# Seven of the eight token-to-channel turns of the input projection taken off TensorE: VectorE 32x32 blocks and a trip through DRAM

## The chip, the core and the metric

The kernel runs on one core of a Trainium2 chip. The metric is the device time of one execution in microseconds (us); before the change the median of three runs is 1167.25 us (1164.77 to 1167.39). Engines are named as in the profile: PE (TensorE matmul), PEld (its weight loads), DVE (VectorE), ACT (ScalarE), POOL (GpSimd), SP (the engine whose queue issues the loads and stores here).

## The reference

One encoder layer on 256 tokens of width 2048, fp32. The part that the change touches is the mixing sub-layer:

```python
hn = rms_norm(h, g_mix_pre)
u = hn @ w_in                                   # 2048 -> 5120
q, k, v, xr, yg = split(u, [1024, 2048, 3072, 4096])
attn = neighborhood_attention(q, k, v, rpb)     # 8 heads of 128, 4 rows x 64 columns of tokens
rec = rglru_bidirectional(xr, ...) * gelu(yg)   # conv of 4 taps, two gates, two scans
mixed = concat(rms_norm(attn), rms_norm(rec)) @ w_out
h = h + rms_norm(mixed)
```

Behind it come a SwiGLU FFN (2048 to 5632 and back) and a gated embedding, each with its norms.

## The kernel before, in words

Every product runs on PE in three passes (`hi*hi`, `hi*lo`, `lo*hi`), since each fp32 operand is split in two parts: ACT rounds the weight tile `wr` to `wh` (L472), DVE subtracts to get `wl` (L501). A weight tile holds 2 x 128 rows and 512 columns and feeds twelve matmuls of 512 columns (L539 to L541 in `products`). There are four raw weight buffers and six pairs `wh`, `wl`, so ACT and DVE can be several tiles ahead of PE.

The input projection is ten chunks of 512 columns, eight weight tiles each, with tokens on the partitions of the result `acc`. Their order was X0, V0, Q0, K0, X1, V1, Q1, K1, G0, G1 (x for the recurrence, v, q, k, and the gate; two halves of each). When a chunk is done, its `post` function runs beside the next chunks: `evac` scales `acc` by the norm into the one buffer `ev` (ACT, L791). x, q, k and the gate are needed with channels on the partitions, and `transposed` does that with four PE transposes into one PSUM bank (L321), two such sets for a chunk. Then:

- x: ACT copies the turned data into `xp` with the tokens in row order (L808); `rec_unit` works on two blocks of 128 channels at a time, four units in all, called units 0 to 3 here (0 and 1 from X0, 2 and 3 from X1). A unit loads its gate weights into `av` (`load_gates`, L821) and splits them (`gh` on ACT L301, `gl` on DVE L303), does eight convolution instructions on DVE (L844, L849: four taps, two blocks), splits the result `xc` (`xch` ACT, `xcl` DVE), and then PE multiplies it by the gate weights (`pg`, two groups of twelve matmuls, L325 to L327). Sigmoids, exponentials, scans and the sum `hs` (L888) follow, and the next unit begins.
- q, k: split into `qh`, `ql`, `kh`, `kl` (L301, L303); then the heads' scores `sc` on PE.
- gate: multiplied into `hs` (L956).

The program is one list for each engine, executed in order. Its order is made by the planner `Plan` while the kernel is built: each piece of work is a generator that yields an engine and an estimated cost, and the piece that could start first is placed next. PE pieces are placed between half weight tiles of the main products, when the planner holds their inputs to be ready. A piece that is late on the chip holds its engine, and so whatever stands behind it.

In the FFN another way of turning is already in use (`Gated.turn`, L1608 to L1645): DVE transposes 32x32 blocks in place, one DMA writes the result to a DRAM buffer `via`, four DMAs read it back with the blocks exchanged, all from SP's queue.

Of the kernel before, what the change touches and what calls it, by code (L numbers as in the profile page):

```python
# [16 lines left out]
P = 128  # L17
# [22 lines left out]
C_RG = 8.0  # L40

# [19 lines left out]
ADDED = 3.0  # L61
LANDED = 6.0
SHARED = 2.6
# [30 lines left out]
class Plan:  # L94
# [13 lines left out]
    def __init__(self, **slots):  # L108
        self.clk = {"act": 0.0, "dve": 0.0, "pe": 0.0, "dma": 0.0, "sum": 0.0}
# [123 lines left out]
def added(kb):  # L233
    return ("sum", kb / 512 * ADDED, None, None, None)


# [5 lines left out]
def layer(ctx: ExitStack, tc: tile.TileContext, a: dict, out: bass.AP):  # L242
# [4 lines left out]
    ps = ctx.enter_context(tc.tile_pool(name="ps", bufs=4, space=bass.MemoryType.PSUM))  # L247
    plan = Plan(
# [74 lines left out]

    def mm3(o, lh, ll, rh, rl, start, stop, shared=False):
# [56 lines left out]
    singles, sums, by_dma = {}, {}, set()  # L381

    class Group:


        def __init__(self, w, n0, lhs, ks, kinds, post, after=None):
# [5 lines left out]
            for (k, _), kind in self.units:  # L392
                i = len(tiles)
                tiles.extend((w[c], k, n0[c]) for c in range(2))
                by_dma.update(i + n for n in {"d": (0, 1), "e": (1,), "c": (0,), "t": (0,)}.get(kind, ()))
                if kind in "st":
# [59 lines left out]
    def hi_stream():  # L456
        for i in range(len(tiles)):
# [16 lines left out]
            if i in by_dma:  # L474
                yield act(2 * N)
                nc.scalar.activation(los[i], f32(his[i]), AF.Copy, scale=-1.0)
                plan.add(add_raw(i), plan.now)

    def add_to(out, src, kb):
        yield added(kb)  # L480
        plan.clk["dma"] = max(plan.clk["dma"], plan.now - ADDED) + SHARED * kb / 512
        nc.gpsimd.dma_start(out, src, accum_op=ALU.add)
        landed = Event()
        landed.t = plan.now + LANDED
        yield landed

    def add_raw(i):
        yield from add_to(los[i], raws[i], 512)
        done(ev_lo[i, 2])
        used(i)  # L490

    def lo_stream():
        for i in range(len(tiles)):
            if i in by_dma:
                continue
# [83 lines left out]
    def run_group(g, flip):  # L579
# [5 lines left out]
        strassens = [n for n, (_, kind) in enumerate(g.units) if kind in "st"]  # L585
        for n, ((_, kx), kind) in enumerate(g.units):
            if kind in "st":
# [153 lines left out]
    def open_p1():  # L741
# [5 lines left out]
        xp = p1.tile([P, HB, S + 4], F32, name="xp")  # L747
        nc.gpsimd.memset(xp[:, :, 0:2], 0.0)
        nc.gpsimd.memset(xp[:, :, S + 2 : S + 4], 0.0)
# [25 lines left out]
    HB = 4  # L775
# [7 lines left out]
    def evac(ch, func, tables):  # L783
# [3 lines left out]
        for t in range(NT):  # L787
            yield act(N, tables, take="ev" if t == 0 else None)
            if e is None:
                e = t1["pool"].tile([P, NT, N], F32, tag="ev", name="ev")  # L790
            nc.scalar.activation(e[:, t, :], ch.accs[t], func, scale=rstd_x[:, t : t + 1])  # L791
        release(ch)
        return e
# [3 lines left out]
    def xr_post(hf):  # L797
        def post(ch):
# [32 lines left out]
    def rec_unit(b0, xp):  # L831
# [7 lines left out]
        for b in range(2):  # L839
            for j in range(4):  # L840
                w = col("conv_w", j * 8 + b0 + b)
                yield dve(S)
                if j == 0:
                    nc.vector.tensor_scalar(  # L844
                        out=xc[:, b, :], in0=xp[:, b, 0:S], scalar1=w,
                        scalar2=col("conv_b", b0 + b), op0=ALU.mult, op1=ALU.add,
                    )
# [101 lines left out]
    def gate_pair(b0, b, e, ev):  # L949
        hs, sq = t1["hs"], t1["sqr", b // 2]  # L950
        tr = yield from transposed(e, b)
        if b == 2:
            plan.free["ev"].append(plan.now)
        h2 = hs[:, b0 + b : b0 + b + 2, :]
        yield dve(2 * S, give="sm")
        nc.vector.tensor_tensor(out=h2, in0=tr, in1=h2, op=ALU.mult)  # L956
# [5 lines left out]
    def yg_post(hf):  # L962
        def post(ch):
            b0 = hf * HB
            e = yield from evac(ch, AF.Gelu_apprx_tanh, GELU)
# [3 lines left out]
            both = [Event() for _ in range(2)]  # L969
            for i in range(2):  # L970
                plan.add(gate_pair(b0, 2 * i, e, both[i]), plan.now)
# [27 lines left out]
    def qk_post(g, which):  # L999
        def post(ch):  # L1000
# [5 lines left out]
            for b in range(0, HB, 2):  # L1006
                tr = yield from transposed(e, b)
                if b == 2:
                    plan.free["ev"].append(plan.now)
                yield from split(hi[:, b : b + 2, :], lo[:, b : b + 2, :], tr, 2 * S, give="sm")  # L1010
# [153 lines left out]
    O_Q, O_K, O_V, O_X, O_G = 0, DA, 2 * DA, 3 * DA, 3 * DA + DR  # L1164
# [205 lines left out]
    kept = ctx.enter_context(tc.tile_pool(name="kept", bufs=1, space=bass.MemoryType.DRAM))  # L1370

# [182 lines left out]
    def quarters(x):  # L1554
        return x.rearrange("p (c n) -> p c n", n=P)

# [29 lines left out]
    class Gated(Seven):  # L1586
# [5 lines left out]
        def late(self, g):  # L1592
# [13 lines left out]
            yield dve(2 * N)  # L1606
            turned = self.both.rearrange("p c t n -> p (c t n)")
            nc.vector.transpose(turned, turned)  # L1608
            plan.free["uv"].append(plan.now)
            if not self.kk0:  # L1610
                self.mid.open()
            raw = self.mid.raw
            there = Event()
            plan.add(self.turn(raw, there), plan.now, TURN_LATE)
            yield there
            i, j = divmod(self.kk0, 8)
            hi, lo = (x[:, j : j + 4, :].rearrange("p b (t a i) -> p t a b i", t=NT, i=32)
                      for x in self.mid.tiles(i))
            raw = raw.rearrange("p a t (b i) -> p t a b i", i=32)
# [10 lines left out]

        def turn(self, raw, there):
            yield dma(512)
            via = kept.tile([P, 4, NT * P], F32, tag="via", name="via", bufs=2)
            nc.sync.dma_start(via, self.both.rearrange("p c t n -> p c (t n)"))
            out = Event()
            out.t = plan.now + VIA
            yield out
            plan.free["mid"].append(plan.now)
            yield dma(512)
            for c in range(4):  # L1640
                nc.sync.dma_start(
                    raw[c * 32 : (c + 1) * 32].rearrange("j a t n -> j a (t n)"),
                    via[:, c, :].rearrange("(a j) n -> j a n", a=4),
                )
            there.t = plan.now + VIA  # L1645
# [45 lines left out]
    for part, (f0, f1) in enumerate(parts):  # L1691
# [4 lines left out]
        for us in units[:1] if last else units:  # L1696
            summed += [k for kind, k in us if kind in "st" and k not in summed]
# [201 lines left out]
```

## Time and profile before

| | |
|---|---|
| median of three runs | 1167.25 us (1164.77, 1167.25, 1167.39) |
| profiled execution: its time | 1164.49 us |
| profiled execution: its span, first to last instruction | 1162.7 us |
| granted TensorE clock, mean | 0.997 |
| PE busy in the span | 98% |
| DVE, ACT busy in the span | 81%, 60% |

The span is the profiled execution of one program; the time holds some 1.8 us more around it. A busy PE is a PE with matmuls in flight: one 512-column matmul is listed with some 390 ns, but the next one starts some 227 ns after it, and this distance is the cost of one. What PE waits for is read from the list of waits, where a wait is put down to the engine that ended it.

### The profile page before, as it was taken

The page shows a single profiled execution, that of the slowest core. Times are in us where ns is not written, and L with a number is a line of the kernel's source. Part 1 is how long each engine was busy: PE and PEld are TensorE (multiplying, and loading weights), DVE is VectorE, ACT ScalarE, POOL GpSimd, SP SyncE. Part 2 cuts the span into 40 slices and gives each one's busy share as a digit, 9 for nine tenths or more (in the row PEclk, how much of TensorE's full clock was granted, in tenths as well). Part 3 has the DMA queues.
Part 4 walks back from the last instruction along what each step waited for, and adds up shares of the span by engine and source line. Part 5 has one row for each costly group of instructions (what it writes and reads, how often), then busy time and mean ns, then how long its engine had stood idle before and what let it go on. Part 6 is the DMA issues. An engine that isn't in the chain of part 4 may idle for free.

```text
span 1162.7 us, 14552 instructions
## 1 busy us (share of the span) xinstructions
PE 1144.1 (98%) x5189; PEld 948.0 (82%) x5189; DVE 942.7 (81%) x1214; ACT 692.2 (60%) x927; POOL 1.6 (0%) x13
## 2 busy tenths in 40 slices
PE   7999999999999999999999999999999999999996
PEld 5888888888888888888888888888888888888885
DVE  6677868778548889899877889989977999987663
ACT  6787877766547645565454555556444546466752
POOL 0000000000000000000000000000000000000000
PEclk9999999999999999999999999999999999999998
DMA  9855565545874967677765676677675667975741
GB/s 311 288 172 184 170 195 183 163 156 171 314 252 142 319 206 239 231 234 240 232 216 171 224 222 199 203 232 255 211 240 177 209 201 216 331 268 168 247 145 73
DMA packets 78265, 250.34 MB, mean 215 GB/s; under 512 B 8433, under 2 KB 20337, under 8 KB 76785
## 3 DMA queue, kind: packets, MB, share of 16 engines
q1 hardware_dynamic: 78048, 249.33, 65.4%
q8 instruction: 41, 0.67, 0.2%
q14 instruction: 32, 0.25, 0.1%
q10 hardware_dynamic: 144, 0.08, 0.0%
HBM read 238.37 MB, written 11.01 MB: 214 GB/s over the span
## 4 chain that ended last, share of the span: by engine, by line
PE 92%; DVE 3%; ACT 2%; DMA 2%; SPq 1%; issue 1%; DVEq 0%; ACTq 0%
PE c L539 14%; PE c L541 14%; PE c L540 14%; PE acc L541 11%; PE acc L540 11%; PE acc L539 11%; PE p L548 3%; PE p L550 3%; PE p L549 3%; PE c L548 2%; PE c L549 2%; PE c L550 2%; DMA av<-in_w_rg_i 1%; DVE wl L501 1%; PE tr L321 1%; ACT wh L472 1%
## 5 line engine op out<-in xcount | busy, mean ns | idle before, releaser
L501 DVE TENSOR_TENSOR wl<-wr,wh 128x1024 fp32r<-128x1024 f32 (+1 forms) x319 | 368.1, 1170 | 87.7 <-ACT wh L472 87.1
L472 ACT CAST wh<-wr 128x1024 fp32r<-128x1024 f32 (+1 forms) x319 | 317.3, 1012 | 164.8 <-PE acc L541 70.5
L539 PE MATMUL c<-wh,hT_mix_hi 128*128 128x512 f32 x436 | 170.1, 390 | 0.0
L541 PE MATMUL c<-wh,hT_mix_lo 128*128 128x512 f32 x436 | 169.7, 389 | 0.0
L540 PE MATMUL c<-wl,hT_mix_hi 128*128 128x512 f32 x436 | 169.6, 389 | 0.0
L472 ACT CAST wh<-lent_t 128x1024 fp32r<-128x1024 f32 x65 | 68.0, 1053 | 117.8 <-DVE lent_t L525 84.4
L539 PE MATMUL acc<-wh,hT_hi 128*128 128x512 f32 x320 | 128.5, 402 | 6.7 <-ACT wh L472 6.7
L540 PE MATMUL acc<-wl,hT_hi 128*128 128x512 f32 x320 | 126.2, 394 | 0.8 <-DVE wl L501 0.8
L541 PE MATMUL acc<-wh,hT_lo 128*128 128x512 f32 x320 | 126.1, 394 | 0.0
L541 PEld LDWEIGHTS c<-wh,hT_mix_lo 128*128 128x128 f32 x436 | 81.8, 188 | 17.2 <-DVE hT_mix_lo L309 0.2
L539 PEld LDWEIGHTS c<-wh,hT_mix_hi 128*128 128x128 f32 x436 | 81.9, 188 | 16.8
L540 PEld LDWEIGHTS c<-wl,hT_mix_hi 128*128 128x128 f32 x436 | 81.9, 188 | 16.7
L501 DVE TENSOR_TENSOR wl<-lent_t,wh 128x1024 fp32r<-128x1024 f32 x65 | 78.1, 1219 | 13.5 <-ACT wh L472 13.2
L472 ACT CAST wh<-lent_r 128x1024 fp32r<-128x1024 f32 (+1 forms) x61 | 58.8, 981 | 32.5 <-PE c L541 25.6
L539 PEld LDWEIGHTS acc<-wh,hT_hi 128*128 128x128 f32 x320 | 61.0, 191 | 18.4 <-ACT wh L472 6.7
L501 DVE TENSOR_TENSOR wl<-lent_r,wh 128x1024 fp32r<-128x1024 f32 (+1 forms) x61 | 68.3, 1129 | 8.3 <-ACT wh L472 8.2
L540 PEld LDWEIGHTS acc<-wl,hT_hi 128*128 128x128 f32 x320 | 60.9, 190 | 13.8 <-DVE wl L501 2.2
L541 PEld LDWEIGHTS acc<-wh,hT_lo 128*128 128x128 f32 x320 | 60.8, 190 | 12.9
L541 PE MATMUL acc<-wh,hT_ffn_lo 128*128 128x512 f32 x112 | 43.7, 390 | 0.4 <-DVE hT_ffn_lo L309 0.4
L539 PE MATMUL acc<-wh,hT_ffn_hi 128*128 128x512 f32 x112 | 44.1, 393 | 0.0
L540 PE MATMUL acc<-wl,hT_ffn_hi 128*128 128x512 f32 x112 | 43.6, 389 | 0.0
L539 PE MATMUL c<-wh,mid1h 128*128 128x512 f32 x88 | 34.2, 389 | 0.0
(440 smaller groups left out, 2219.1 us busy)
## 6 DMA issues: line engine op xcount, KB each, us to landing
wr<-in_w_in SPq DMA_DIRECT2D x79, 512.0 KB, 4.3
wr<-in_w_ffn_down SPq DMA_DIRECT2D x70, 512.0 KB, 4.6
wr<-in_w_ffn_gate SPq DMA_DIRECT2D x64, 512.0 KB, 4.6
wr<-in_w_ffn_up SPq DMA_DIRECT2D x64, 512.0 KB, 4.2
wr<-in_w_out SPq DMA_DIRECT2D x32, 512.0 KB, 4.7
wr<-in_w_ple_gate SPq DMA_DIRECT2D x32, 512.0 KB, 4.5
lent_r<-in_w_ffn_up SPq DMA_DIRECT2D x24, 512.0 KB, 4.7
lent_r<-in_w_ffn_gate SPq DMA_DIRECT2D x24, 512.0 KB, 4.5
```

The costliest lines, as they stand in the source:

```text
L321: nc.tensor.transpose(tr[:, b, t * P : (t + 1) * P], src, ident)
L472: nc.scalar.copy(his[i][:, j, :], raws[i][:, j, :])
L501: nc.vector.tensor_tensor(out=los[i][:, j, :], in0=raws[i][:, j, :], in1=f32(his[i][:, j, :]), op=ALU.subtract,)
L539: nc.tensor.matmul(accs[t], hi[t], wh[:, j, :], start=st, stop=False)
L540: nc.tensor.matmul(accs[t], hi[t], wl[:, j, :], start=False, stop=False)
L541: nc.tensor.matmul(accs[t], lo[t], wh[:, j, :], start=False, stop=sp)
L548: nc.tensor.matmul(o, lh, wh, start=start, stop=False)
L549: nc.tensor.matmul(o, lh, wl, start=False, stop=False)
L550: nc.tensor.matmul(o, ll, wh, start=False, stop=stop)
```

## The change

x, q, k and the first gate half (G0) are turned as in the FFN. `evac` now writes `ev` in quarters of 128 columns; `turned` adds one DVE block transpose of 128x1024; `turn` adds the write to `via` and four reads back into `ev`, on SP's queue. The columns of `w_in` are permuted on the host in 32s, so that the exchange comes out right. One ACT copy or split of 1024 elements then reads `ev` in place of two of 512 that read PSUM. In `xp` the tokens stay in column order; the convolution taps are shifted by `j * NR`, two small DVE copies fill the edges between rows, and the convolution writes `xc` in row order itself, which makes `xc` a strided operand (neighbours 64 elements apart, runs of four). G1 and the heads' own transposes stay on PE. V1 now stands behind Q1 and K1. Code for a kind of tile that no table uses (`by_dma`, `added`) is removed, and the planner's `LANDED` goes from 6.0 to 2.5.

```diff
+    def turned(e, raw, read, free=None):
+
+        yield dve(2 * N)
+        flat = e.rearrange("p c t n -> p (c t n)")
+        nc.vector.transpose(flat, flat)
+        plan.add(turn(e, raw, read, free), plan.now, TURN_LATE)
+
+    def turn(e, raw, read, free):
+        yield dma(512)
+        via = kept.tile([P, 4, NT * P], F32, tag="via", name="via", bufs=2)
+        nc.sync.dma_start(via, e.rearrange("p c t n -> p c (t n)"))
+        out = Event()
+        out.t = plan.now + VIA
+        yield out
...
+        yield dma(512)
+        for c in range(4):
+            nc.sync.dma_start(
+                raw[c * 32 : (c + 1) * 32].rearrange("j a t n -> j a (t n)"),
+                via[:, c, :].rearrange("(a j) n -> j a n", a=4),
+            )
+        read.t = plan.now + VIA
...
-            for b in range(0, HB, 2):
-                tr = yield from transposed(e, b)
-                if b == 2:
-                    plan.free["ev"].append(plan.now)
-                yield act(2 * S, give="sm")
-                nc.scalar.copy(
-                    xp[:, b : b + 2, 2 : S + 2].rearrange("p b (r c) -> p b r c", r=NR),
-                    tr.rearrange("p b (c r) -> p b r c", r=NR),
+            yield act(4 * S)
+            nc.scalar.copy(by_block(xp[:, :, LEFT : LEFT + S]), e)
...
+                to = xc[:, b, :].rearrange("p (r c) -> p c r", r=NR)
+                src = xp[:, b, j * NR : j * NR + S].rearrange("p (c r) -> p c r", r=NR)
...
                     nc.vector.scalar_tensor_tensor(
-                        out=xc[:, b, :], in0=xp[:, b, j : j + S], scalar=w, in1=xc[:, b, :],
-                        op0=ALU.mult, op1=ALU.add,
+                        out=to, in0=src, scalar=w, in1=to, op0=ALU.mult, op1=ALU.add,
                     )
...
-            for b in range(0, HB, 2):
-                tr = yield from transposed(e, b)
-                if b == 2:
-                    plan.free["ev"].append(plan.now)
-                yield from split(hi[:, b : b + 2, :], lo[:, b : b + 2, :], tr, 2 * S, give="sm")
+            yield from split(by_block(hi), by_block(lo), e, 4 * S, give="ev")
...
         (O_X, xr_post(0)), (O_V, v_post(0)), (O_Q, qk_post(0, "q")), (O_K, qk_post(0, "k")),
-        (O_X + N, xr_post(1)), (O_V + N, v_post(1)), (O_Q + N, qk_post(1, "q")),
-        (O_K + N, qk_post(1, "k")), (O_G, yg_post(0)), (O_G + N, yg_post(1)),
+        (O_X + N, xr_post(1)), (O_Q + N, qk_post(1, "q")),
+        (O_K + N, qk_post(1, "k")), (O_V + N, v_post(1)), (O_G, yg_post(0)), (O_G + N, yg_post(1)),
```

What the planner makes of it is seen in the order of the instructions. On PE, before, in the second chunk (V0, its result is `acc_363` and `acc_364`), the two sets that turn X0 stand between matmuls of the main product:

```order
L541 MATMUL acc_364<-wh,hT_lo 128x512
L321 MATMUL tr<-ident,ev 128x128 x4
L539 MATMUL acc_363<-wh,hT_hi 128x512
L540 MATMUL acc_363<-wl,hT_hi 128x512
L541 MATMUL acc_363<-wh,hT_lo 128x512
L539 MATMUL acc_364<-wh,hT_hi 128x512
L540 MATMUL acc_364<-wl,hT_hi 128x512
L541 MATMUL acc_364<-wh,hT_lo 128x512
L321 MATMUL tr<-ident,ev 128x128 x4
```

After the change these sets are gone, and so are those of X1, Q0, Q1, K0, K1 and G0: fourteen sets. The first gate group `pg` of unit 0 stands behind 21.5 weight tiles, where it stood behind 17.5 (counted in PE's order); here it is in the new order, in the third chunk (Q0):

```order
L550 MATMUL acc_554<-wh,hT_lo 128x512
L354 MATMUL pg<-xch,gh 128x256
L355 MATMUL pg<-xcl,gh 128x256
L356 MATMUL pg<-xch,gl 128x256
```

On DVE, in the new order, between the first convolution of unit 1 and its gate weights stand a block transpose (that of K0) and a weight split:

```order
L867 TENSOR_SCALAR xc<-xp,vec 128x64x4
L872 SCALAR_TENSOR_TENSOR xc<-xp,vec,xc 128x64x4
L327 STREAM_TRANSPOSE ev<-ev 128x1024
L872 SCALAR_TENSOR_TENSOR xc<-xp,vec,xc 128x64x4 x2
L867 TENSOR_SCALAR xc<-xp,vec 128x64x4
L872 SCALAR_TENSOR_TENSOR xc<-xp,vec,xc 128x64x4 x2
L510 TENSOR_TENSOR wl<-wr,wh 128x1024
L872 SCALAR_TENSOR_TENSOR xc<-xp,vec,xc 128x64x4
L299 TENSOR_TENSOR gl<-av,gh 128x1024
L299 TENSOR_TENSOR xcl<-xc,xch 128x512
```

Before, the same place held the eight convolutions, one weight split, `gl` and `xcl`; what moved in is the transpose, and the convolutions have the strided form.

On SP's queue, in the new order, the trip of Q0 stands between weight loads, and behind it come the gate weights of unit 1:

```order
L333 DMA via<-ev 128x1024
L475 DMA wr<-in_w_in 128x1024 x2
L341 DMA ev<-via 32x4x256 x4
L475 DMA wr<-in_w_in 128x1024 x5
L842 DMA av<-in_w_rg_a 128x2x128
```

Before, there was no `via` on this stretch of the queue. Behind the first half of the output projection PE's, ACT's and DVE's instructions stand in the same order as before.

## Rows read from the trace of the kernel before

**Rows 1.** The page's first part: busy time, share of the span, instructions.

```profile
PE 1144.1 (98%) x5189; PEld 948.0 (82%) x5189; DVE 942.7 (81%) x1214; ACT 692.2 (60%) x927; POOL 1.6 (0%) x13
```

**Rows 2.** Windows, the stretch of the input projection and the first tiles behind it.

```profile
core 0: us, PE busy (x) PEld busy (x) DVE busy (x) ACT busy (x) POOL busy (x), PEclk, DMA share, GB/s
9.60:290.00 280.40, 278.71 (x1354) 232.74 (x1354) 214.59 (x323) 206.80 (x315) 0.00 (x0) 1.00 0.61 197
```

**Rows 3.** Waits of PE: line and who ended them, us in total, times, longest.

```profile
PE acc L539 <- ACT wh L472: 6.7, 1, 6.7
PE pg L326 <- DVE xcl L303: 0.9, 3, 0.5
PE acc L540 <- DVE wl L501: 0.8, 1, 0.8
```

**Rows 4.** Timeline of PE: start, duration, instruction; one transposing set of X0.

```profile
47.70 0.39 PE L540 MATMUL acc<-wl,hT_hi 128*128 128x512 f32 x1
47.93 0.39 PE L541 MATMUL acc<-wh,hT_lo 128*128 128x512 f32 x1
48.16 0.60 PE L321 MATMUL tr<-ident,ev 128*128 128x128 f32 x4
48.51 0.47 PE L539 MATMUL acc<-wh,hT_hi 128*128 128x512 f32 x1
48.83 0.39 PE L540 MATMUL acc<-wl,hT_hi 128*128 128x512 f32 x1
49.05 0.39 PE L541 MATMUL acc<-wh,hT_lo 128*128 128x512 f32 x1
```

**Rows 5.** Timeline of DVE and ACT: the FFN's first and last turn, from transpose to reader.

```profile
411.56 1.25 DVE L1608 STREAM_TRANSPOSE mid<-mid 128x1024 f32<-128x1024 f32 x1
425.34 1.05 ACT L301 CAST mid0h<-turned 128x1024 fp32r<-128x1024 f32 x1 [3.50 <-DMA turned<-via]
...
995.05 1.25 DVE L1608 STREAM_TRANSPOSE mid<-mid 128x1024 f32<-128x1024 f32 x1
1006.60 1.05 ACT L301 CAST mid2h<-turned 128x1024 fp32r<-128x1024 f32 x1 [0.71 <-DMA turned<-via]
```

**Rows 6.** Timeline of ACT: the second copy into `xp` of X0.

```profile
51.17 0.58 ACT L808 COPY xp<-tr 128x512 f32<-128x512 f32 x1
```

**Rows 7.** Groups by line and shape, 0 to 300 us: convolution, strided sum, plain product.

```profile
L849 DVE SCALAR_TENSOR_TENSOR xc<-xp,vec,xc 128x256 f32<-128x256 f32 x24 | 11.6, 484 | 0.7
L914 DVE TENSOR_TENSOR ig<-ig,r 128x512 f32<-128x512 f32 x8 | 5.2, 686 | 1.0 <-ACT r L911 0.7
L888 DVE TENSOR_TENSOR hs<-th 128x512 f32<-128x512 f32 x4 | 4.3, 1078 | 0.1
```

**Rows 8.** Timeline of DVE and PE at unit 0; in brackets the idle time before.

```profile
58.78 1.23 DVE L303 TENSOR_TENSOR gl<-av,gh 128x1024 fp32r<-128x1024 f32 x1 [2.87 <-ACT gh L301]
60.74 0.39 PE L326 MATMUL pg<-xcl,gh 128*128 128x256 f32 x1 [0.46 <-DVE xcl L303]
```

**Rows 9.** Timeline of DVE and PE at unit 1.

```profile
101.47 0.68 DVE L303 TENSOR_TENSOR xcl<-xc,xch 128x512 fp32r<-128x512 f32 x1
102.72 0.28 PE L325 MATMUL pg<-xch,gh 128*128 128x256 f32 x1
```

**Rows 10.** Timeline of DVE and PE at units 2 and 3.

```profile
151.53 1.23 DVE L303 TENSOR_TENSOR gl<-av,gh 128x1024 fp32r<-128x1024 f32 x1 [2.41 <-ACT gh L301]
153.41 0.39 PE L326 MATMUL pg<-xcl,gh 128*128 128x256 f32 x1 [0.23 <-DVE xcl L303]
191.29 0.39 PE L326 MATMUL pg<-xcl,gh 128*128 128x256 f32 x1 [0.20 <-DVE xcl L303]
```

**Rows 11.** Timeline of DVE and PE: the last split of k and the scores behind it.

```profile
218.66 0.69 DVE L303 TENSOR_TENSOR kl<-tr,kh 128x512 fp32r<-128x512 f32 x1 [0.77 <-ACT kh L301]
220.10 0.23 PE L325 MATMUL sc<-kh,qh 128*128 128x160 f32 x1
```

More of the change, by code (lines that the diff above doesn't have):

```diff
@@ L40 @@
 C_RG = 8.0
+O_X = 3 * DA
 VEC_COLS = {}
@@ L60 @@
 MM = 0.2267
-ADDED = 3.0
-LANDED = 6.0
-SHARED = 2.6
+LANDED = 2.5
 VIA = 1.5
@@ L379, in seg @@
         segs.append(s)
-    singles, sums, by_dma = {}, {}, set()
+    singles, sums = {}, {}
     class Group:
@@ L584, in run_group @@
         i = g.i0
-        strassens = [n for n, (_, kind) in enumerate(g.units) if kind in "st"]
+        strassens = [n for n, (_, kind) in enumerate(g.units) if kind == "s"]
         for n, ((_, kx), kind) in enumerate(g.units):
-            if kind in "st":
+            if kind == "s":
                 seven(i, kx, g, n == strassens[0], n == strassens[-1])
@@ L789, in evac @@
             if e is None:
-                e = t1["pool"].tile([P, NT, N], F32, tag="ev", name="ev")
-            nc.scalar.activation(e[:, t, :], ch.accs[t], func, scale=rstd_x[:, t : t + 1])
-        release(ch)
-        return e
+                e = t1["pool"].tile([P, 2 * N], F32, tag="ev", name="ev")
+                if turns:
+                    e = e.rearrange("p (c t n) -> p c t n", c=4, t=NT)
+                else:
+                    e = e.rearrange("p (t n) -> p t n", t=NT)
+            to, src = (e[:, :, t, :], quarters(ch.accs[t])) if turns else (e[:, t, :], ch.accs[t])
+            nc.scalar.activation(to, src, func, scale=rstd_x[:, t : t + 1])
+        release(ch)
+        if not turns:
+            return e
+        read = Event()
+        raw = e.rearrange("p c t n -> p (c t n)").rearrange("p (a t n) -> p a t n", a=4, t=NT)
+        yield from turned(e, raw, read)
+        yield read
+        return by_token(raw)
     ev_rec = [Event() for _ in range(5)]
@@ L950, in gate_pair @@
         hs, sq = t1["hs"], t1["sqr", b // 2]
-        tr = yield from transposed(e, b)
-        if b == 2:
-            plan.free["ev"].append(plan.now)
         h2 = hs[:, b0 + b : b0 + b + 2, :]
-        yield dve(2 * S, give="sm")
-        nc.vector.tensor_tensor(out=h2, in0=tr, in1=h2, op=ALU.mult)
+        if e is not None:
+            tr = yield from transposed(e, b)
+            if b == 2:
+                plan.free["ev"].append(plan.now)
+            yield dve(2 * S, give="sm")
+            nc.vector.tensor_tensor(out=h2, in0=tr, in1=h2, op=ALU.mult)
         yield act(2 * S)
@@ L964, in post @@
             b0 = hf * HB
-            e = yield from evac(ch, AF.Gelu_apprx_tanh, GELU)
+            e = yield from evac(ch, AF.Gelu_apprx_tanh, GELU, not hf)
             yield ev_rec[hf + 1]
@@ L969, in post @@
             both = [Event() for _ in range(2)]
+            if not hf:
+                h4 = by_block(t1["hs"][:, b0 : b0 + HB, :])
+                yield dve(4 * S)
+                nc.vector.tensor_tensor(out=h4, in0=e, in1=h4, op=ALU.mult)
+                plan.free["ev"].append(plan.now)
             for i in range(2):
-                plan.add(gate_pair(b0, 2 * i, e, both[i]), plan.now)
+                plan.add(gate_pair(b0, 2 * i, e if hf else None, both[i]), plan.now)
             for ev in both:
@@ L1611, in late @@
                 self.mid.open()
[L1612 to L1615, printed above, removed]
+            raw, read = self.mid.raw, Event()
+            yield from turned(self.both, raw, read, "mid")
+            yield read
             i, j = divmod(self.kk0, 8)
-            hi, lo = (x[:, j : j + 4, :].rearrange("p b (t a i) -> p t a b i", t=NT, i=32)
-                      for x in self.mid.tiles(i))
-            raw = raw.rearrange("p a t (b i) -> p t a b i", i=32)
+            hi, lo = (by_block(x[:, j : j + 4, :]) for x in self.mid.tiles(i))
+            raw = by_token(raw)
             yield from split(hi, lo, raw, 2 * N)
@@ L1629, in late @@
                     )
[L1631 to L1645, printed above, removed]
         def sum_up(self, g, n, t, c, x, ev):
@@ L1696, in layer @@
         for us in units[:1] if last else units:
-            summed += [k for kind, k in us if kind in "st" and k not in summed]
+            summed += [k for kind, k in us if kind == "s" and k not in summed]
         mid.ev_sums = {k: Event() for k in summed}
@@ L1880 @@
         k, m = w.shape
+        if n == "w_in":
+            w = w.copy()
+            for n0 in (O_X, O_X + N, 0, N, DA, DA + N, O_X + DR):
+                sl = slice(n0, n0 + N)
+                w[:, sl] = w[:, sl].reshape(k, 4, 4, 32).transpose(0, 2, 1, 3).reshape(k, N)
         if n == "w_ffn_down":
```

63 lines of the change are left out of this document (25 added, 38 removed).

## The prediction

> **What bounds the kernel now.** I read the shares of busy time first. PE is busy for 1144.1 of 1162.7 us [rows 1], so the question is whether it ever waits. The list of PE's waits answers it: 6.7 us at the start for the first weight tile, and behind that 0.9 us for `xcl` and 0.8 us for a `wl` [rows 3]. In the stretch that the change rewrites PE is busy for 278.7 of 280.4 us, at the full clock, while DVE is busy for 215 and ACT for 207 [rows 2]. So PE sets the time: what leaves PE is gained in full, what makes PE wait is lost in full, and work on DVE, ACT and the queues costs nothing until something that PE waits for is late.
>
> The PE timeline prices what leaves. Matmuls of 512 columns start 0.23 us apart (47.70 and 47.93; 48.83 and 49.05 [rows 4]). Around a set of four transposes the starts are 47.93, 48.51 and 48.83: 0.58 and 0.32 in place of 0.23 each. A set costs PE 0.35 + 0.09, rounded 0.45 us, although its row says 0.60.
>
> **What leaves PE.** Seven chunks of two sets: 14 x 0.45 = 6.3 us. The products, the heads' transposes and G1's sets stay. Behind the input projection the order of the engines is unchanged, and PE already waited for almost nothing there, so this gain is carried to the end.
>
> At this place a rule of the Trainium skill speaks against the change. VectorE: DVE Perf Modes, section "Rules for kernel authors", advises TensorE for a 128x128 transpose whose result may go to PSUM, and VectorE only for single 32x32 blocks. By that rule the change would lose; it looks at one transpose's own duration, while the rows show that here PE's time is the scarce one. What it has right is the latency, weighed next.
>
> **What is added beside PE.** Seven block transposes on DVE of 1.25 us each [rows 5] are 8.8 us, into a stretch in which DVE is idle for 280.4 - 214.6 = 66 us [rows 2]. The ACT copies and splits of 1024 elements read in runs of 32, as the FFN's casts of `turned` do, at 1.05 us [rows 5]; two of 512 take 2 x 0.58 [rows 6]: nothing added. Seven trips move 1 MB each, 7.3 MB over 280 us, 26 GB/s beside the 197 in that stretch [rows 2]. SP holds the weight loads behind a trip while `via` lands; four raw buffers and six split ones lie between a load and its matmul, 2.7 us of PE each (12 x 0.227), so I let a few us of that cost nothing. Without that cover each blocked us would show as a wait of `acc` for `wh`.
>
> **What gets late, and where PE meets it.** The turned data come later: in the FFN 13.8 us from the start of the block transpose to the reader for the first turn, and 11.5 for the last, of eleven [rows 5]. Before, X0's way through PE took 3.6 us (48.16 [rows 4] to 51.75, the end of the second copy [rows 6]). With a turn of 11.5, a copy of 1.05 and two small edge copies (estimate 0.3, from the smallest operations around them) it takes 12.9: 9.3 us later. PE meets it at unit 0's `pg`, which moved from 17.5 to 21.5 weight tiles: 4 x 2.72 less the two missing sets, 10.0 us later. So a typical turn is just in time, and one of 13.8 is 1.6 us late. That holds for units 0 and 2, and for the scores of both halves, where the old room was about 0.75 us (`kl` ended at 219.35, the scores began at 220.10 [rows 11]). I take 0.25 us at each of the four places, 1.0 us; the bounds are 0 and 2.3 us each (13.8 against 11.5).
>
> The second thing that gets late is the convolution. It now writes and re-reads `xc` with neighbours 256 bytes apart. No row of before has that form. The nearest is the sum `hs`, whose output has a stride of 16 bytes: 1078 ns for 512 elements, where a plain product takes 686 [rows 7]. That is 0.39 us for 512, so 0.2 for the convolution's 256, on top of 0.484 [rows 7]. Bounds: nothing, and twice that, 0.4, if the strided input is paid for as well. I take 0.2, since every element of `hs` already falls apart from its neighbour. The planner's cost for these instructions is as before, so PE's places don't allow for it. Eight in a unit: 1.6 us.
>
> The Trainium skill has a rule for this price: SBUF — State Buffer, section "Door 1: The DMA port swizzle", says that SBUF is accessed in lines of 16 bytes and that an access to a new line pays a penalty unless the line is hit at least twice. The trace agrees with it at `hs` (1078 against 686). By it a stride of 256 bytes is no worse than one of 16, an estimate of the same 0.2, and the read side of `xc` would pay too.
>
> Where do these 1.6 us fall? In units 0 and 2 DVE stood idle for 2.87 and 2.41 us ahead of `gl`, because the gate weights arrived last [rows 8, 10]; the convolution grows into that: 0. In unit 1 there was no such gap: `xcl` ended at 102.15 and PE came at 102.72 [rows 9], 0.6 us of room, so 1.0 us shows. In unit 3 PE already waited 0.20 us for `xcl` [rows 10]; all 1.6 shows. The block transpose that stands amid unit 1's convolutions is in the planner's costs, so I add nothing for it; if the planner had not covered it, unit 1 would be 1.25 us later still.
>
> V1 behind K1 brings the second scores two chunks after X1's turn rather than three; K1's data are needed 6.5 tiles (17.7 us) after its chunk ends, as against 15.0 us in the first half, so it costs nothing. `LANDED` and the removed code left the order of the FFN as it was: nothing.
>
> **The sum.** Against the profiled execution: 1164.5 - 6.3 + 1.0 (four turns) + 1.0 (unit 1) + 1.6 (unit 3) = 1161.8 us. The profiled execution was the fastest of four (1164.49, 1164.77, 1167.25, 1167.39; mean 1166.0, median of the three timed ones 1167.25). I put the new median 1.5 us above the sum, as the mean stands to the profiled one: **1163.3 us**. A difference of 0.3%, 3.5 us (1163.75), is about what a measurement of this kernel can tell from none, so the likeliest case lies at that border.
>
> **The rivals.**
> - The late work is hidden after all: the strided convolution costs nothing extra, or the planner's half-tile places leave room for it. Then 6.3 is gained and up to 0.9 of old waits on `xcl` with it [rows 3]: 1157.3 to 1159 against the profiled execution, a median near 1159.5. For it: DVE's 66 idle us, and a planner whose places were missed by at most 0.46 us [rows 8, 10]. Against it: two of those places were missed with cheaper convolutions. Chance 0.27.
> - The turns are late by 1 us more than I take, at each of the four places: 4 us more, so 1165.8 and a median near 1167: no change. For it: the first FFN turn needed 13.8, and its reader stood idle for it for 3.5 us [rows 5]. Against it: PE never waited for such a turn in the FFN, though there it is far behind. Chance 0.21. This is also the way in which the skill's advice for TensorE would come out.
> - The other side, slower: the convolution with its 256-byte stride. With x us more for a unit, 4x less the room (0.6 + 2.9 + 2.4) plus 1.0 for the turns is PE's added wait; it passes 6.3 at x = 2.8 (0.35 us a convolution) and makes the kernel slower by 3.5 us at x = 3.7 (0.46 a convolution, 0.95 us in all). Then 1168 and a median of 1169 to 1170. For it: out and in both strided, in four units out of four on the chain to `pg`. Against it: the 16-byte stride costs 0.2, and twice that is still below 0.46. Chance 0.10.
>
> **How the numbers follow.** My forecast has 0.42, with a range of its own from 1161 to 1166 (convolutions between 0.1 and 0.3 dearer, turns between 0 and 0.5 late); a little over half of it lies below 1163.75. Faster: 0.27 + 0.23 = 0.50. Within 0.3%: 0.19 + 0.21 = 0.40. Slower: 0.10. The range of 8 in 10 runs from 1158 (below it the best part of the first rival) to 1168.5 (above it the third).
>
> **What would show it.** `tr<-ident,ev` should fall from 64 to 8 matmuls, and PE's busy time in the input projection by about 6. The convolution's group should read about 680 ns in place of 484; below 520 the first rival holds, above 900 the third. PE's waits should name `pg` for `xcl` or `gl` with 2 to 5 us in all, most of it at units 1 and 3, and `sc` for `kl` with less than 1. The turns should take 10 to 14 us. Windows behind the input projection should be unchanged but shifted. I am wrong in kind if PE waits for `wh` or `wl` there: then SP's queue, held by the trips, starves the weight loads, which I priced at nothing. I am also wrong if a piece that the new order placed behind a late turn on DVE or ACT holds up weight splits for longer than the six pairs cover.

## The result, and the profile after

The changed kernel takes 1168.57 us (median of 22 runs, 1164.48 to 1173.69); the kernel before, beside it, 1165.7 (22 runs). The ratio is 1.0022, 95% interval 1.0012 to 1.0032: slower by about 2.6 us, where the prediction had 1163.3 and faster. The profiled execution was the longest of the 22: 1173.69 us, span 1171.8. So what it shows is more than typical; a second profile follows in experiment 12.

The first part of the page, and the window that answers to [rows 2]:

```profile
PE 1144.3 (98%) x5133; PEld 946.5 (81%) x5133; DVE 956.3 (82%) x1220; ACT 689.0 (59%) x919; POOL 1.6 (0%) x13
```

```profile
9.60:290.00 280.40, 270.28 (x1260) 224.23 (x1259) 219.00 (x317) 198.37 (x301) 0.00 (x0) 0.98 0.70 218
```

56 matmuls are gone (5189 to 5133), as many as 14 sets of four. But in the same 280 us PE is now idle for 10.1 us where it was idle for 1.7, and the granted clock, the third column from the right, is 0.98 in place of 1.00. PE's busy total over the whole program did not fall with the matmuls (1144.1 and 1144.3), mainly because a matmul at the lower clock is busy for longer: behind unit 0 the starts of 512 columns lie 0.43 us apart (76.69 and 77.11), where they lay 0.23 apart before [rows 4]. The groups by line show the set and the convolution (mean ns behind the bar; [rows 7] has 484):

```profile
L872 DVE SCALAR_TENSOR_TENSOR xc<-xp,vec,xc 128x256 f32<-128x256 f32 x24 | 16.5, 689 | 0.7
...
L327 DVE STREAM_TRANSPOSE ev<-ev 128x1024 f32<-128x1024 f32 x7 | 8.7, 1238 | 2.0 <-ACT ev L805 2.0
...
L317 PE MATMUL tr<-ident,ev 128*128 128x128 f32 x8 | 1.3, 287 | 0.6 <-ACT ev L805 0.6
```

PE's waits, against [rows 3]:

```profile
PE acc L548 <- ACT wh L500: 6.9, 1, 6.9
PE pg L354 <- ACT gh L297: 1.9, 1, 1.9
PE pg L354 <- ACT xch L297: 1.5, 1, 1.5
PE acc L549 <- DVE wl L510: 1.5, 2, 0.9
PE acc L548 <- ACT attn_hi L297: 1.1, 1, 1.1
PE sc L354 <- ACT kh L297: 1.1, 1, 1.1
PE sc L355 <- DVE kl L299: 0.9, 1, 0.9
PE pg L356 <- DVE gl L299: 0.8, 1, 0.8
PE pg L355 <- DVE xcl L299: 0.7, 1, 0.7
```

Behind the start they are 10.5 us in all (two smaller ones of 1.0 together are left out), where before had 2.1 (1.7 of it in [rows 3]). PE's timeline says where: unit 0 (72.91, 74.18), unit 1 (118.29, 119.37) and the scores of the second half (209.37, 210.62). Units 2 and 3 wait for nothing.

```profile
72.91 0.39 PE L354 MATMUL pg<-xch,gh 128*128 128x256 f32 x1 [1.94 <-ACT gh L297]
74.18 0.39 PE L356 MATMUL pg<-xch,gl 128*128 128x256 f32 x1 [0.75 <-DVE gl L299]
...
118.29 0.38 PE L354 MATMUL pg<-xch,gh 128*128 128x256 f32 x1 [1.51 <-ACT xch L297]
119.37 0.58 PE L355 MATMUL pg<-xcl,gh 128*128 128x256 f32 x1 [0.70 <-DVE xcl L299]
...
209.37 0.34 PE L354 MATMUL sc<-kh,qh 128*128 128x160 f32 x1 [1.10 <-ACT kh L297]
210.62 0.34 PE L355 MATMUL sc<-kl,qh 128*128 128x160 f32 x1 [0.92 <-DVE kl L299]
```

Right behind each of the three pairs the clock falls. One-microsecond windows behind unit 0 (columns as in [rows 2]; PEclk is the third from the right):

```profile
74.00:75.00 1.00, 0.82 (x5) 0.82 (x6) 1.00 (x2) 0.98 (x2) 0.00 (x0) 0.74 0.81 299
75.00:76.00 1.00, 1.00 (x6) 1.00 (x6) 1.00 (x2) 1.00 (x1) 0.00 (x0) 0.50 0.26 102
76.00:77.00 1.00, 1.00 (x5) 0.90 (x4) 1.00 (x2) 0.99 (x4) 0.00 (x0) 0.50 0.42 94
77.00:78.00 1.00, 1.00 (x4) 0.74 (x4) 0.53 (x1) 0.27 (x1) 0.00 (x0) 0.56 0.96 340
78.00:79.00 1.00, 1.00 (x6) 0.82 (x5) 0.00 (x0) 0.36 (x1) 0.00 (x0) 1.00 0.97 238
```

Such a drop to 0.50 (1.2 in place of 2.4 GHz) loses the sum of one minus the clock over its windows, 0.26 + 0.50 + 0.50 + 0.44 = 1.7 us. The three of this execution lose 5.1 us. Before has no such drop in the input projection. Against before's profiled execution the span grew by 9.1 us: 6.3 less for the sets, 8.4 more of waits, 5.1 of clock are 7.2. Most of the other 1.9 us are found in the traces. A wait is listed from the end of the matmul ahead of it, but the next matmul would have started 0.16 us before that end (0.39 and 0.23 us behind its start [rows 4]), and seven waits more than before make 1.1 us of this. And the fourteen sets, taken one by one on PE's timeline of before, cost 5.9 us and not 6.3: ten cost 0.45 each, two beside a gate group 0.33 each and G0's two 0.77 together. Some 0.4 us stay without a place.

How unit 0 came to be late, on DVE and ACT:

```profile
51.48 1.24 DVE L327 STREAM_TRANSPOSE ev<-ev 128x1024 f32<-128x1024 f32 x1
64.61 1.05 ACT L824 COPY xp<-ev 128x1024 f32<-128x1024 f32 x1 [4.35 <-DMA ev<-via]
65.98 0.52 DVE L867 TENSOR_SCALAR xc<-xp,vec 128x256 f32<-128x256 f32 x1
71.29 0.62 ACT L297 CAST xch<-xc 128x512 fp32r<-128x512 f32 x1 [3.73 <-DVE xc L872]
71.81 1.04 ACT L297 CAST gh<-av 128x1024 fp32r<-128x1024 f32 x1
72.30 0.69 DVE L299 TENSOR_TENSOR xcl<-xc,xch 128x512 fp32r<-128x512 f32 x1
72.90 1.22 DVE L299 TENSOR_TENSOR gl<-av,gh 128x1024 fp32r<-128x1024 f32 x1
```

The turn takes 13.1 us to its reader and the convolution starts 14.5 us behind the transpose. `xch` is now what comes last, and `gh` on ACT and `gl` on DVE stand behind the splits of `xc`; before, `gl` came last because it waited for the gate weights, with 2.87 us idle ahead of it [rows 8].

Unit 1 is late in another way:

```profile
100.77 1.05 ACT L297 CAST qh<-ev 128x1024 fp32r<-128x1024 f32 x1 [2.79 <-DMA ev<-via]
105.70 1.29 DVE L936 TENSOR_TENSOR ig<-ig,r 128x512 f32<-128x512 f32 x2 [0.35 <-ACT r L933]
```

ACT stood idle for 2.79 us until Q0's trip had brought the data for `qh` (14.2 us behind the block transpose at 86.60). Behind `qh` on ACT stand the last step of unit 0's `r` (105.04), behind that on DVE unit 0's `ig`, scans and sum, and only then the convolutions of unit 1 (110.29 on). So Q0's turn lies on the chain to unit 1's `pg` as well.

### The profile page after: what moved, and what is told of

Read it like the earlier page. It is cut to its first block, busy times and chain, and to the rows that moved or that the text cites. A ratio compares the mean times of both kernels' runs of the same rounds, so it can differ in the third digit from the quotient of the medians.

```text
span 1171.8 us, 14500 instructions
## 1 busy us (share of the span) xinstructions
PE 1144.3 (98%) x5133; PEld 946.5 (81%) x5133; DVE 956.3 (82%) x1220; ACT 689.0 (59%) x919; POOL 1.6 (0%) x13
## 4 chain that ended last, share of the span: by engine, by line
PE 80%; DVE 7%; DMA 6%; ACT 3%; issue 2%; SPq 1%; DVEq 0%; ACTq 0%
PE c L548 14%; PE c L550 14%; PE c L549 14%; PE acc L548 7%; PE acc L550 7%; PE acc L549 7%; PE p L557 3%; PE p L559 3%; PE p L558 3%; DMA wr<-in_w_in 3%; PE c L559 2%; PE c L558 2%; PE c L557 2%; DVE wl L510 2%; ACT wh L500 1%
## 5 line engine op out<-in xcount | busy, mean ns | idle before, releaser
L549 PEld LDWEIGHTS acc<-wl,hT_hi 128*128 128x128 f32 x320 | 61.7, 193 | 15.3 <-DVE wl L510 3.4
```

The costliest lines, as they stand in the source:

```text
L549: nc.tensor.matmul(accs[t], hi[t], wl[:, j, :], start=False, stop=False)
```

## The experiments

Three theories at first. **A**: the strided convolution makes units 0 and 1 late. **B**: the turns through DRAM are late by themselves. **C**: the new order of the chunks (V1 behind Q1 and K1) does it. Ratios are to the kernel before in the same rounds (1165.84, 1165.29 and 1165.86 us in the three sets), with 95% intervals.

**1. A contiguous convolution in the changed kernel.** The tokens stay in column order, so the reordering is left out.

```diff
-                to = xc[:, b, :].rearrange("p (r c) -> p c r", r=NR)
-                src = xp[:, b, j * NR : j * NR + S].rearrange("p (c r) -> p c r", r=NR)
+                to = xc[:, b, :]
+                src = xp[:, b, j * NR : j * NR + S]
```

> The changed kernel with the convolution's operands contiguous, in the same order of instructions; the output then leaves out the reordering of the tokens, so only its time is read. Theory A, the strided convolution makes unit 0 and unit 1 late: the group falls from 689 to about 484 ns, PE's waits for the gate products of units 0 and 1 (4.9 us in the profile of the changed kernel) fall by 1.6 us each or vanish, the clock stays at full speed behind them, and the median falls by 4 to 6 us, to 1162.5 to 1164.5. Theory B, the late turns through DRAM are the cause and the convolution's length is hidden: the group falls as well but the waits stay, the median stays within 1 us of 1168.6. Theory C, the new order of the chunks is the cause: as B.

Measured: 1162.85 us, ratio 0.9977 (0.9966 to 0.9987), 5.7 below the changed kernel. The convolution reads 483 ns. PE's timeline at units 0 and 1, and DVE's `gl` of unit 0:

```profile
70.87 1.23 DVE L299 TENSOR_TENSOR gl<-av,gh 128x1024 fp32r<-128x1024 f32 x1 [0.51 <-ACT gh L297]
70.89 0.39 PE L354 MATMUL pg<-xch,gh 128*128 128x256 f32 x1 [0.76 <-ACT gh L297]
72.15 0.38 PE L356 MATMUL pg<-xch,gl 128*128 128x256 f32 x1 [0.76 <-DVE gl L299]
115.09 0.39 PE L355 MATMUL pg<-xcl,gh 128*128 128x256 f32 x1 [0.23 <-DVE xcl L299]
```

Against the changed kernel 1.17 us less at unit 0, 1.98 less at unit 1, and none at the second scores; one clock drop (1.7 us) remains, behind unit 0. The time is the one that A expected. The 1.5 us at unit 0 are left over without the stride, and not the turn's alone: `gh` started 0.51 us late for the gate weights, which are loaded behind the trip on SP's queue, and DVE still stood idle for 0.51 us ahead of `gl`, of the 2.87 before [rows 8]. At unit 1 the chain from the first convolution to `xch` is 1.4 us shorter than in the changed kernel; the rest of the 1.98 goes with Q0's trip, which took 12.7 us here and 14.2 there.

**2. The planner told of the longer convolution.** Nothing else changes; PE's places for the units move back.

```diff
-                yield dve(S)
+                yield dve(580)
```

> The changed kernel with the planner told that a convolution takes 0.68 us in place of 0.35; the work is the same, only the places change (the first gate group of unit 1 moves from 35.5 to 37 weight tiles, that of unit 0 from 21.5 to 22). Theory A: PE's waits at units 0 and 1 fall from 4.9 to below 1.5 us and the median by 3 to 5 us, to 1163.5 to 1165.5. Theory B: unit 0, half a tile later, still waits about 1.4 us less than before at most, unit 1 as before; median within 2 us of 1168.6.

Measured: 1166.64 us, ratio 1.0012 (1.0003 to 1.0021). Units 0 and 1 no longer wait, but the waits come back later, at unit 2 (`xch`, `xcl`) and at the end of the input projection, where the one clock drop now is. So the waits at units 0 and 1 went as A expected, but the time did not come down to A's range; it lies at the edge of B's:

```profile
PE acc L548 <- ACT attn_hi L297: 3.3, 1, 3.3
...
PE pg L354 <- ACT xch L297: 1.4, 1, 1.4
PE pg L355 <- DVE xcl L299: 0.7, 1, 0.7
```

**3. The planner told of a longer turn** in the input projection (2.5 tiles a transfer in place of 1.5).

```diff
-        out.t = plan.now + VIA
+        out.t = plan.now + (VIA if free else VIA1)
...
-        read.t = plan.now + VIA
+        read.t = plan.now + (VIA if free else VIA1)
```

> The changed kernel with the planner told that each of the two transfers of a turn takes 1 us longer, 2 us for a turn, in the input projection alone; the work is the same, the first gate groups move one tile later (21.5 to 22.5, 35.5 to 36.5) and the second scores from 62.5 to 63 tiles. Theory B, late turns: the waits at unit 0 and at the second scores (4.7 us in all in the profile) vanish, median 1162 to 1164.5. Theory A: unit 0 gains the same tile and so loses its wait, unit 1 gains one too, but the scores' wait of 2 us stays; median 1164 to 1166. Both theories expect a gain, the places tell them apart.

Measured: 1163.57 us, ratio 0.9981 (0.9972 to 0.9990). The convolution is as slow as before this edit (687 ns). Unit 0 waits 1.58 + 0.70, unit 1 0.68, the second scores 1.11; one drop is left. The edit also changed the order on SP's queue: the four reads of X0's trip stand three weight loads behind its write in place of two, and the turn took 16.3 us (49.97 to 66.30), so unit 0, placed a tile later, gained little. `qh` no longer waited for its trip, and unit 1 gained most. Planning the turn gives back 5.0 us, but not at the places that either theory named.

**4. The order of the chunks alone**, on the kernel before.

```diff
-        (O_X + N, xr_post(1)), (O_V + N, v_post(1)), (O_Q + N, qk_post(1, "q")),
-        (O_K + N, qk_post(1, "k")), (O_G, yg_post(0)), (O_G + N, yg_post(1)),
+        (O_X + N, xr_post(1)), (O_Q + N, qk_post(1, "q")),
+        (O_K + N, qk_post(1, "k")), (O_V + N, v_post(1)), (O_G, yg_post(0)), (O_G + N, yg_post(1)),
```

> The kernel before with V1 moved behind Q1 and K1 and nothing else. Theories A and B: within 1.5 us of the kernel before (1165.7), PE's waits in the input projection below 2.5 us. Theory C, the order of the chunks crowds the second scores and unit 3 together: 2 us or more slower than before, with waits at the scores.

Measured: 1164.81 us, ratio 0.9995 (0.9986 to 1.0004), no clock drop. C falls.

**5. The reordering moved to ACT.** The convolution is contiguous again, and four strided ACT copies put the turned x into row order. It computes everything.

```diff
-            nc.scalar.copy(by_block(xp[:, :, LEFT : LEFT + S]), e)
...
+            for b in range(HB):
+                yield act(S)
+                nc.scalar.copy(
+                    xp[:, b, LEFT : LEFT + S].rearrange("p (r t a x) -> p t a x r", r=NR, t=NT, a=4),
+                    e[:, :, :, b, :].rearrange("p t a (x r) -> p t a x r", r=NR),
+                )
```

> The changed kernel, but the token reordering of x moves from the convolution to the ACT copy that reads the turned data: four strided copies of 256 elements per x chunk in place of one of 1024 and two edge copies, and the convolution reads and writes neighbours again. It computes everything. Theory A (the strided convolution is what made units 0 and 1 late): convolutions back to about 485 ns (from 689), waits of pg at units 0 and 1 of 1.7 us or less in sum (from 5), the clock drop at unit 1 gone, 1162 to 1164 us, as with the contiguous convolution that leaves the reordering out (1162.85). Price of the copies: the old copy of 512 strided elements took 0.58, so four of 256 take about 1.4 us where one of 1.05 stood: at most 0.4 us later. Theory B (the long turn alone makes the units late): the waits of pg stay at 4 us or more and the time at 1167 to 1169.

Measured: 1162.50 us, ratio 0.9979 (0.9964 to 0.9995): faster than before and about 6 us below the changed kernel. The waits behind the start, and the copies of X0 (four in 2.10 us, where one of 1024 took 1.05):

```profile
PE acc L549 <- DVE wl L510: 1.3, 1, 1.3
PE acc L548 <- ACT attn_hi L297: 1.0, 1, 1.0
PE pg L355 <- DVE xcl L299: 0.8, 2, 0.5
...
PE pg L356 <- DVE gl L299: 0.2, 1, 0.2
```

```profile
61.19 2.10 ACT L825 COPY xp<-ev 128x256 f32<-128x256 f32 x4 [1.83 <-DMA ev<-via]
```

No drop in this execution, which is the fastest of twelve (1159.99 to 1169.43). Beside before's profiled one it agrees with the price of the sets: 1159.99 against 1164.49 is 4.5 us less, and 6.3 (or 5.9) less 1.6 of added waits (3.7, with 0.4 for `hT_ffn_lo`, against 2.1) is 4.7 (or 4.3). The medians differ by only 2.8 us. The copies cost 0.7 us more than I expected; DVE waited 0.3 us for them, and PE at unit 0 no more than 0.2.

**6. The same with the longer turn planned** (experiments 5 and 3 together).

> As the run with the reordering on ACT, and the planner is told that a turn of the input projection takes longer (2.5 tiles for each of its two transfers). With theory A and a late turn as the smaller second cause: no wait of pg above 0.5 us, the second scores' wait of 1 us may stay, 1161 to 1163 us. If moving PE's places only moves the waits to the end of the input projection (attn_hi, 3.3 us when the convolution's true cost was planned): 1163 to 1165, no better than without it. Theory B: 1163 or less as well, so this run tells the causes apart only beside the other one.

Measured: 1162.31 us, ratio 0.9975 (0.9965 to 0.9985). `pg` still waits 2.8 us in four pieces, the longest 1.0, so the expected half microsecond was missed. X0's turn took 16.2 us, as in experiment 3, and behind unit 0's two waits of 0.79 and 0.70 us the clock fell again (to 0.50 until 81.0, 1.7 us lost). No gain over experiment 5 can be told.

**7. Both true costs planned in the changed kernel** (experiments 2 and 3 together).

> The changed kernel as it is on the engines, but the planner is told both true costs: the convolution at 0.68 us in place of 0.3, and the longer turn. Theory A plus B: PE's places for the units move 2 to 6.5 tiles back, so the waits at pg and sc vanish (from 7 us to below 1) and so do the three clock drops; what is left over is the end, where attn_hi waited 3.3 us when only the convolution's cost was planned: 3 to 6 us there. 1163 to 1167 us. If the waits at pg stay with both costs planned, neither late convolutions nor late turns cause them and a queue behind them on ACT or DVE does: 1167 to 1169.

Measured: 1172.04 us, ratio 1.0055 (1.0043 to 1.0068), the slowest of all and outside both expectations. The waits at `pg` and `sc` did go (0.3 us left), but the end of the input projection became late: this row at 279, with a clock drop behind it that lost 1.7 us, which was not expected either, and five waits of 4.0 us together between 261 and 294. All other groups behind the start, these five among them, are 7.8 us.

```profile
PE acc L549 <- ACT ev L806: 3.9, 1, 3.9
```

**8. x turned on PE again**, q, k and G0 through DRAM; ten of the fourteen sets stay off PE.

```diff
-            e = yield from evac(ch, AF.Copy, COPY)
+            e = yield from evac(ch, AF.Copy, COPY, False)
...
+                tr = yield from transposed(e, b)
```

> Only q, k and the first gate half go through DRAM; x is turned by PE as before, with the old copies and convolution. 10 of 14 sets leave PE, 4.5 us by the price of 0.45 a set. Both theories: no wait of pg for xch, xcl or gl above 0.5 us. Theory A or B alike then gives before's time less 4.5 plus the second scores' wait (0 to 2 us, and 1.7 of clock if it reaches 2): 1161 to 1164 us. If it comes out at 1165 or above, the price of a set or the cost of the remaining trips on the queues is wrong, and the waits would be for wh or wl, or at sc.

Measured: 1163.67 us, ratio 0.9987 (0.9978 to 0.9996), no drop, `pg` waits 1.1 us in all, 0.8 of it at one `gl` (expected: 0.5 at most).

**9. The strided convolution alone**, on the kernel before: all turns on PE, only the convolution's operands as in the changed kernel, so that the tokens are then in another order than the rest takes them to be.

```diff
-                        out=xc[:, b, :], in0=xp[:, b, j : j + S], scalar=w, in1=xc[:, b, :],
+                        out=to, in0=src, scalar=w, in1=to,
```

> The kernel before, with only the convolution's operands laid out as in the changed kernel (output and running sum with neighbours 256 bytes apart); the tokens then stand in another order than the rest takes them to be. All transposes stay on PE and nothing is turned through DRAM. The convolution should read about 690 ns. By the prediction's step (the gap ahead of gl hides it in units 0 and 2; unit 1 pays 1.0 and unit 3 1.6): 2.6 us of waits of pg, at units 1 and 3 alone, and 2.6 us slower than before. By the rival (the stride was ruinous only together with a late turn, whose lateness had used the room up): 1 us or less at each unit, no clock drop, and no more than 2.6 us slower. By theory A at its strongest (the stride alone costs what undoing it gave back): 5 us or more slower, with waits at units 0 and 2 as well.

Measured: 1167.41 us, ratio 1.0013 (1.0004 to 1.0022), no drop. The convolution reads 691 ns. PE waits at unit 1 and unit 3, and hardly at units 0 and 2 (0.02 and 0.11 us). At unit 0 the convolution grew into DVE's idle time ahead of `gl`:

```profile
59.61 1.23 DVE L303 TENSOR_TENSOR gl<-av,gh 128x1024 fp32r<-128x1024 f32 x1 [1.45 <-ACT gh L301]
...
104.42 0.39 PE L326 MATMUL pg<-xcl,gh 128*128 128x256 f32 x1 [0.64 <-DVE xcl L303]
...
194.30 0.39 PE L326 MATMUL pg<-xcl,gh 128*128 128x256 f32 x1 [1.67 <-DVE xcl L303]
```

That is the prediction's own step, in kind and nearly in size (1.0 and 1.6). Alone, the stride costs about 1.5 us. Experiment 1 says that the turns without the stride gain 2.7 us (0.23%). Added, the two would make the kernel 1.2 us faster; together they made it 2.6 us slower. Nearly 4 us (some 2 to 6 by the three intervals) belong to neither alone.

**10 and 11. A wait of known size**, on the kernel before: three or five needless DVE products in unit 1, unknown to the planner, ahead of the splits. What is shown is the edit of 10; 11 has `range(5)`.

```diff
+        if b0 == 2:
+            for _ in range(3):
+                nc.vector.tensor_tensor(out=xcl, in0=xc, in1=xc, op=ALU.mult)
         yield from split(xch, xcl, xc, 2 * S)
```

> The kernel before, with three needless products of 512 elements (about 0.6 us each) put on DVE in unit 1 ahead of its splits and unknown to the planner; nothing else is changed. xcl, which had 0.6 us of room, comes 1.8 us later: PE should wait 1.0 to 1.4 us at unit 1's pg. Both theories of the clock (a wait of 2 us also halves PE's clock for 3.5 us; or the drops seen in the changed kernel have another cause) expect no drop for a wait this short: 1.0 to 1.4 us slower than before.

> As the run with the short wait, with five needless products: PE should wait 2.2 to 2.7 us at unit 1's pg. If a wait of 2 us by itself brings the clock down, the granted clock behind it reads 0.50 for 3.4 us, 1.7 us are lost beside the wait and the kernel is 3.9 to 4.4 us slower than before. If the drops of the changed kernel came from its DMA trips or its other operations, the clock stays at 1.00 and the kernel is 2.2 to 2.7 us slower.

Measured: 1167.98 us, ratio 1.0020 (1.0012 to 1.0029), and 1170.64 us, ratio 1.0032 (1.0020 to 1.0044). The wait at unit 1 was 1.40 us in 10 and 2.87 us in 11. Windows of 10, then of 11, at its end and behind it:

```profile
104.00:106.00 2.00, 1.13 (x9) 1.13 (x10) 2.00 (x4) 0.77 (x2) 0.00 (x0) 1.00 0.00 0
106.00:108.00 2.00, 2.00 (x12) 1.70 (x12) 2.00 (x2) 1.99 (x3) 0.00 (x0) 1.00 0.49 98
```

```profile
106.00:108.00 2.00, 0.39 (x3) 0.39 (x4) 2.00 (x3) 0.00 (x0) 0.00 (x0) 1.00 0.00 0
108.00:110.00 2.00, 2.00 (x11) 2.00 (x11) 2.00 (x3) 1.27 (x1) 0.00 (x0) 0.52 0.34 29
110.00:112.00 2.00, 2.00 (x7) 1.52 (x7) 2.00 (x2) 1.24 (x4) 0.00 (x0) 0.62 0.72 258
```

After the short wait the clock stays at 1.00. After the long one it is near 0.5 until about 111.5, with 1.7 us lost (0.96 and 0.76 in the two windows), in a kernel that has no trips in its input projection. The profiled executions differ by 1170.75 - 1167.00 = 3.75 us, with 1.47 us more wait at unit 1, 0.4 more at a set of X0 and 1.7 of clock. So a wait brings the clock down without a trip beside it.

**12. The changed kernel once more.**

> The changed kernel once more, unchanged, since its first profiled execution was the longest of 22 by 1.9 us. If the three clock drops of that execution belong to the kernel, this profile shows two or three again, at units 0 and 1 and the second scores; if they were that execution's own, it shows fewer, the waits of pg and sc read 5 us or less in sum, and the span is 1164 to 1168 us.

Measured: 1169.45 us (1165.10 to 1176.67), ratio 1.0036 (1.0018 to 1.0054). This profile, too, comes from a long execution (span 1172.6) and shows units 0 and 1 late again; the third drop is at `attn_hi`, not at the scores. Unit 1 is later than in the first profile, as is `qh`, by the same 0.7 us:

```profile
PE pg L354 <- ACT xch L297: 2.4, 1, 2.4
PE pg L354 <- ACT gh L297: 1.8, 1, 1.8
...
PE sc L355 <- DVE kl L299: 1.4, 1, 1.4
PE acc L548 <- ACT attn_hi L297: 1.1, 1, 1.1
```

```profile
101.43 1.05 ACT L297 CAST qh<-ev 128x1024 fp32r<-128x1024 f32 x1 [3.70 <-DMA ev<-via]
```

The drops lose 6.8 us here. How many there are varies: by the mean clock listed for each of the first 22 runs, clock lost (one minus clock, by the span) has a median of 5.8 us, against 3.5 for the kernel before (30 runs), so a typical execution pays about 2.3 us of it, not 5. That is rough, since the listed clock has three decimals, 1.2 us of this span.

## Why the prediction was wrong, point by point

- **What leaves PE: right.** 14 sets; one by one in the trace of before they cost 5.9 us, and the profiled execution of experiment 5 agrees with either 5.9 or 6.3 to 0.2 us.
- **The price of the strided convolution: right.** 689 against 484 ns, 0.2 us, in the middle of its bounds. The two of eight that do not re-read `xc` (L867) rose by 0.11 only, from 406 to 514 ns, so a unit pays 1.45 us and not 1.6. The rule on lines of 16 bytes in the Trainium skill (SBUF — State Buffer, section "Door 1: The DMA port swizzle") led to the same estimate, and the trace agrees with it.
- **Where the 1.6 us fall: this step failed.** "In units 0 and 2 DVE stood idle for 2.87 and 2.41 us ahead of `gl` ...; the convolution grows into that: 0." That is true while the convolution is the only thing late (experiment 9). With the turn it is not. The prediction wrote the turn's lateness and the convolution's as two terms and set each against the room that the trace of before showed, though they stand on one chain and have one room between them. At unit 0 DVE's idle time ahead of `gl` was 2.87 us before, 1.45 with the stride alone (experiment 9), 0.51 with the turns alone (experiment 1) and none with both; the turns without the stride already cost 1.5 us of wait there, and the stride then came through with 1.2. At unit 1 the prediction had no turn at all, but Q0's turn holds ACT ahead of it: the room of 0.6 us was gone already without the stride (0.23 us of wait in experiment 1); with it the wait is 2.2, and 2.9 in the second profile, not 1.0.
- **The turns, 0.25 us at each of four places: wrong in size.** They took 13.1 us at X0, 14.2 at Q0 and 15.3 at the second K (193.02 to 208.27; 13.1 in the second profile), not 11.5. The waits are 1.5 at unit 0 without the stride and 1.4 to 2.0 at the second scores; the first scores and unit 2 wait for none. Why the second K's trip varies so (12.1 us in experiment 1), and whether the stride has a part in the second scores' wait, which experiment 1 does not have, was not tried.
- **Unit 3, 1.6 us: none.** Nor does unit 2 wait, although with the planner's new places of experiment 2 it does. Which of the moved places gave the room was not tested apart.
- **A term that was missing: the clock.** The sum priced a wait at its own length. Behind nine of the ten waits of 2 us or more, in one or two pieces, that these traces have behind the start, the clock fell, mostly at a cost of another 1.7 us: about 2.3 us in a typical execution of the changed kernel and 5.1 in the profiled one.
- **V1's place, nothing: right** (experiment 4). **Waits for `wh` and `wl`:** behind the start the first none, the second 1.5 us against 0.8, so SP's queue did not starve PE.
- **`attn_hi`, 1.1 us: not foreseen.** It stands in the changed kernel and experiments 1 and 5 alike, and grows to 3.3 when the units are placed later; what makes it was not tried apart.
- **The rivals.** The second (turns later by 1 us at four places) named the direction, and 1167 is near; but the time came from two or three places, and the undoing of the stride alone gave back 5.7 us. The third asked for convolutions of 0.46 us more; 0.2 sufficed, since the room was spent.

As for the rule of the Trainium skill that speaks for TensorE (VectorE: DVE Perf Modes, "Rules for kernel authors"): the changed kernel came out its way, but not because the turns left PE, since experiment 5 takes the same turns off PE and is faster than before (0.9979).

## What to carry to other kernels

Room is a property of a chain, not of a step: where two edits delay the same chain, add their delays first and subtract the room once. When a layout change can be paid for on either of two engines, put it on the one that is not on the way to the engine that sets the time, as the strided copy on ACT instead of the strided convolution on DVE. Telling a planner the true cost of late work is no sure gain: the turn's cost alone gave back 5.0 us here, the convolution's alone 1.9, and both together lost 3.5, as the waits moved to the end of the stage and grew; why they did was not tried.

## What the runs showed of the hardware

A wait of PE can cost more than its length. After one of 2.87 us, made by needless products in experiment 11, the granted clock fell to 0.50 for some 3.4 us and 1.7 us were lost; after one of 1.40 us in experiment 10, and one of 1.67 in experiment 9, it stayed at 1.00. In the changed kernel pairs of waits of 2.7, 2.2 and 2.0 us did it. The pair of 2.1 us at unit 2 in experiment 2 did not, and 1.5 us in two pieces at unit 0 in experiments 1 and 6 did, so between these ends the length alone doesn't tell. The drop can also last longer: behind unit 1 in experiment 12 it went on for some 7 us and lost 3.4, with only the 0.50 us for `xcl` as a further wait in it.

The same trip can differ from one execution of a kernel to the next: the second K's took 15.3 and 13.1 us in the two profiles of the changed kernel, Q0's 14.2 and 15.1.
